# The last head of the first attention stays in SBUF, and the first token block's operands are made inside the attention

## The chip, the cores and the metric

The kernel runs on one core of a Trainium2 chip. The metric is the device time of one execution in microseconds (us). A core has a matrix engine (PE, with its weight loads as PEld), a vector engine (DVE), a scalar engine (ACT), a general engine (POOL), and queues that issue transfers (DMAs) between the chip's large memory (HBM) and the on-chip memory (SBUF); nearly all of this kernel's transfers are issued from SyncE's queue (SP). Matmul results land in PSUM, banks of 128 x 512 float32.

## The reference, cut to what matters

The program is a two-layer encoder over 1024 tokens of width 1024. Layer 0 mixes tokens by multi-head latent attention, layer 1 by differential attention; each mixer and each SwiGLU is followed by a scaled residual and a layer norm. The change lies between the first attention and its output projection:

```python
def block(args):                                # 128 queries at a time, 8 heads
    i, qn_b, qr_b = args
    logits = (jnp.einsum('bqhd,bkhd->bhqk', qn_b, k_nope) + jnp.einsum('bqhd,bkd->bhqk', qr_b, k_rope))
    logits = jnp.where(_chunk_mask(i * Q_BLOCK, s), logits * scale, NEG_BIG)
    p = jax.nn.softmax(logits, axis=-1)
    return jnp.einsum('bhqk,bkhd->bqhd', p, v)
...
o = _from_blocks(o).reshape(b, s, MLA_HEADS * MLA_V)
return o @ w_o
...
h = _layernorm(ALPHA * h + mix, ln_mix_g[i], ln_mix_b[i])
```

## The kernel before, in words

**Numbers.** Every float32 matmul is made of three matmuls of a shorter format: an operand is split into a high part (a cast on ACT) and a low part (a subtraction on DVE or POOL), and the product is high x high + high x low + low x high (`mm3`, lines 143 to 145). So each operand costs a cast and a subtraction before PE can use it.

**The first attention** goes head by head over eight query blocks of 128 tokens. For a block, `softmax_block` makes the scores on PE (s_a, line 216), adds the mask and takes the extreme on DVE (line 219), takes the exponential on ACT (line 222), and POOL multiplies by the reciprocal of the sum (line 1145); all of this lies in a tile `l` of a pool of four buffers. `transpose_block` then transposes the block on PE into PSUM (pt, line 148), and splits it into pth (ACT, line 243) and ptl (DVE, line 244). For two blocks together, `pv_group` multiplies with the values (o_a, line 255; a group g is the pair of blocks 2g and 2g+1), and `mix_a` copies the result out of PSUM (ob, ACT, line 1155) and stores it to HBM (o_dr, line 1156). The last head, head 7, takes its blocks in the order `LAST_ORDER` = 6, 7, 4, 5, 2, 3, 0, 1. A table `fill` names what is done between blocks: projections for the next heads and the like.

**The output projection**, `out_proj`, first loads the eight 128 x 1024 pieces of w_o (r_wo), each split by ACT (line 136) and POOL (line 137). Then, for each token block in `LAST_ORDER`, it fetches all eight heads' outputs of the block from HBM (of, line 299), splits them (ACT line 302, DVE line 303), fetches the block's input rows (zy, line 306), multiplies by w_o (zp_a, 48 matmuls of 128 x 512), adds the residual (line 314), and does the layer norm, whose rows mg and mb POOL's own queue fetches (line 152). Meanwhile the first feed-forward weights (gp) are fetched and split (op_gp, lines 474 and 475).

**What sets the order.** The program is recorded once, and a planner that simulates a time line then fixes one order of instructions for each engine and each DMA queue, so far as the data allow. On the chip each engine works through its list in that order: an instruction that waits holds up those behind it on its engine. A tile's buffer is taken over by the next tile when all readers of the old one are done. In the planned order, the fetch of the first block (block 6) stands on SP behind head 7's store of the group of blocks 6 and 7; the split of block 6's operands stands on ACT ahead of the last pth casts of blocks 0 to 3, and on DVE ahead of their last ptl subtractions; PE's last groups o_a for blocks 2, 3 and 0, 1 need those, and the projection's first matmul stands behind both groups.

Of the kernel before, what the change touches and what calls it, by code (L numbers as in the profile page):

```python
# [9 lines left out]
F32 = mybir.dt.float32  # L10
# [6 lines left out]
P = 128  # L17
# [25 lines left out]
def trunk(  # L43
# [234 lines left out]
    def out_proj(side, w_o, o_dram, x_src, x_dst, lng, lnb, xo):  # L278


        with tc.tile_pool(name="op0", bufs=2, side=side, reuse_waits="tile") as pool:
            g = bcast_row(pool, lng, D, "mg0", "g")
            b = bcast_row(pool, lnb, D, "mb0", "b")
            wo = []
            for h in range(H):
                dst = ()
                if h in (0, 1, 2, 3, 7):
                    t = big_tile(f"wo0_{h}")
                    dst = (t[:, 0], t[:, 1])
                elif h == 6:  # L290
                    t = pool.tile([P, 2, D], F32R, tag=f"wo{h}", name=f"wo0_{h}", bufs=1)
                    dst = (t[:, 0], t[:, 1])
                wo.append(load_w(w_o[h], 1024, f"wo0_{h}", *dst))
            prev = None
            for tb in LAST_ORDER:
                nm = f"a0_{tb}"
                of = pool.tile([P, H, P], F32, tag="of", name=f"of_{nm}", bufs=2)
                src = o_dram[tb // 2][:, :, (tb % 2) * P:(tb % 2) * P + P]
                nc.sync.dma_start(of, src.rearrange("h p q -> p h q"))
                ot = pool.tile([P, 2, D], F32R, tag="oh", name=f"oh_{nm}").rearrange("p a (h q) -> p a h q", h=H)  # L300
                oh, ol = ot[:, 0], ot[:, 1]
                A.copy(oh, of)
                V.tensor_tensor(ol, of, f32(oh), ALU.subtract)
# [757 lines left out]

    with ast as st:
# [88 lines left out]
        def mix_a(h, g):  # L1151
            hc = slice((h % 2) * P, (h % 2) * P + P)
            po = pv_group(pts.pop((h, g)), g, lambda j: tuple(v[:, hc] for v in vt[h // 2, j]), f"a{h}_{g}")
            ob = vp.tile([P, 256], F32, tag="ob", name=f"ob{h}_{g}", bufs=2)
            A.copy(ob, po[:, :256])
            nc.sync.dma_start(o_dr[0][g][h], ob)

# [24 lines left out]
        at(12, constants)  # L1182
        attention(score_a, turn_a, mix_a, fill, 2, (0, 0))
# [13 lines left out]
    def next_x():  # L1197
        pool = xst.enter_context(tc.tile_pool(name="xp0", bufs=1, side="right", reuse_waits="tile"))
        wts["v", 0] = [load_w(w_b_v[0, kh], 1024, f"wbv0_{kh}") for kh in range(2)]
        return new_xT(pool, "f0")  # L1200

    xo, stacks = x_pools("m0", "right")
    pending = out_proj("left", w_o_a, o_dr[0], x, xs_dr[0], ln_mix_g[0], ln_mix_b[0], xo)
# [289 lines left out]
```

## Time and profile before

| | us |
|---|---|
| median of three runs | 2299.32 |
| lowest and highest | 2297.55, 2300.04 |
| the profiled execution | 2302.24 |
| its span, from the first to the last instruction | 2300.2 |
| PE busy | 2253.4 |
| DVE busy | 1551.7 |
| ACT busy | 1017.8 |
| POOL busy | 863.9 |
| first matmul of the output projection, from the span's start | 353.69 |

A profile's row in a timeline gives the start in us, the length in us, the engine, the line of the kernel, the operation, what it writes and reads, shapes and count, and in brackets how long its engine had been idle and who ended that. In a table of stretches each engine has its busy time and, in brackets, the number of its instructions; then come the clock granted to PE (1.00 is full), the DMA engines' busy share, and GB/s. Names are the program's, without buffer numbers: pth_a is the high part of a transposed block of the first attention.

### The profile page before, as it was taken

Reading aid. Unit: us, or ns where it says so; the run is one execution under the profiler, and the core shown is the slowest. Engines: PE = TensorE matmul, PEld = TensorE weight load, DVE = VectorE, ACT = ScalarE, POOL = GpSimd, SP = SyncE. Lnnn points to the kernel's source line nnn. Section 1 sums busy time; section 2 is a strip of 40 time slices with the busy share of each in tenths; the row PEclk is TensorE's granted clock in tenths of the full one; section 3 lists DMA queues with packets and bytes.
Section 4 is the critical chain, followed back from the end, with each engine's and each line's share of the span. In section 5 each row is a group of like instructions: output and inputs, shape, how many; then the busy total and the mean of one; then the engine's idle time right before and its main releaser. Section 6 shows DMA issues by size and latency. Waiting matters only on the chain. (4 is left out here: it accounts for less than half of the span.)

```text
span 2300.2 us, 31168 instructions
## 1 busy us (share of the span) xinstructions
PE 2253.4 (98%) x11410; PEld 1919.6 (83%) x11410; DVE 1551.7 (67%) x2891; ACT 1017.8 (44%) x2096; POOL 863.9 (38%) x688
## 2 busy tenths in 40 slices
PE   8999999999999999999999999999999999999997
PEld 8899997878888887888888898987778888887886
DVE  5667664596666668667476667576586666658777
ACT  4455573342333324445365656555442333324453
POOL 2223241014444445555432424221014444435564
PEclk9999999999999999999999999999999999999999
DMA  5010125434435338544310212053344232337453
GB/s 200 14 36 30 41 72 180 138 128 142 178 133 197 128 111 327 198 171 156 94 54 19 70 38 69 16 214 139 108 160 149 76 120 87 125 127 284 160 205 121
DMA packets 105545, 288.28 MB, mean 125 GB/s; under 512 B 7968, under 2 KB 30112, under 8 KB 94896
## 3 DMA queue, kind: packets, MB, share of 16 engines
q1 hardware_dynamic: 100976, 275.87, 33.5%
q0 software_dynamic: 4416, 10.42, 1.7%
q8 instruction: 90, 1.47, 0.3%
q14 instruction: 63, 0.52, 0.1%
HBM read 205.00 MB, written 77.07 MB: 123 GB/s over the span
## 5 line engine op out<-in xcount | busy, mean ns | idle before, releaser
L474 ACT CAST op_g<-gr 128x512 fp32r<-128x512 f32 x240 | 147.0, 621 | 376.5 <-PE gb L520 188.4
L475 POOL TENSOR_TENSOR op_g<-gr,op_g 128x512 fp32r<-128x512 f32 x104 | 144.0, 1390 | 254.2 <-ACT op_g L474 140.7
L475 DVE TENSOR_TENSOR op_h<-rh,op_h 128x512 fp32r<-128x512 f32 x154 | 157.8, 1055 | 68.2 <-ACT op_h L474 68.2
L520 PE MATMUL ga<-xh_m,op_g 128*128 128x512 f32 x512 | 168.1, 389 | 0.0
L474 ACT CAST op_h<-rh 128x512 fp32r<-128x512 f32 x154 | 92.7, 619 | 147.5 <-PE dx L790 41.1
L790 PE MATMUL dw<-op_w_t,op_h 128*128 128x512 f32 x660 | 151.1, 390 | 0.0
L790 PEld LDWEIGHTS dw<-op_w_t,op_h 128*128 128x128 f32 x660 | 123.6, 188 | 25.6
L222 ACT ACTIVATE l_b<-l_b,mx_b 128x256 f32<-128x256 f32 (+7 forms) x128 | 99.5, 778 | 78.9 <-DVE mx_b L219 77.1
L1297 POOL TENSOR_SCALAR l_b<-l_b,r_b,cst 128x128 f32<-128x128 f32 (+3 forms) x64 | 52.8, 824 | 204.1 <-DVE r_b L224 193.5
L790 PE MATMUL dx<-op_w_b,op_h 128*128 128x512 f32 x528 | 124.4, 397 | 5.0 <-ACT op_w_b L474 3.9
L475 POOL TENSOR_TENSOR op_w_t<-tt,op_w_t 128x512 fp32r<-128x512 f32 x66 | 98.6, 1497 | 80.5 <-ACT op_w_t L474 79.9
L790 PEld LDWEIGHTS dx<-op_w_b,op_h 128*128 128x128 f32 x528 | 101.1, 192 | 28.0 <-ACT op_w_b L474 4.7
L475 DVE TENSOR_TENSOR op_g<-gr,op_g 128x512 fp32r<-128x512 f32 x136 | 111.4, 821 | 17.6 <-ACT op_g L474 17.4
L520 PE MATMUL gc<-b22h_f,op_g 128*128 128x512 f32 x352 | 115.6, 389 | 2.5 <-ACT op_g L474 2.5
L520 PE MATMUL gb<-t3h_f,op_g 128*128 128x512 f32 x352 | 115.6, 390 | 2.2 <-ACT tmp L622 1.6
L520 PE MATMUL gb<-t4h_f,op_g 128*128 128x512 f32 x352 | 115.8, 390 | 1.3 <-DVE tmp L603 1.3
L475 POOL TENSOR_TENSOR op_g<-s,op_g 128x512 fp32r<-128x512 f32 x40 | 54.6, 1365 | 166.0 <-ACT op_g L474 158.0
L520 PE MATMUL gc<-t1h_f,op_g 128*128 128x512 f32 x352 | 115.9, 390 | 0.6 <-ACT op_g L474 0.5
L520 PE MATMUL gb<-t2h_f,op_g 128*128 128x512 f32 x352 | 115.2, 390 | 0.4 <-DVE op_g L475 0.4
L520 PEld LDWEIGHTS ga<-xh_m,op_g 128*128 128x128 f32 x512 | 96.1, 188 | 20.0
L143 PE MATMUL bp<-xT_f,h_wb 128*128 128x512 f32 x256 | 103.7, 405 | 0.0
L145 PE MATMUL bp<-xT_f,l_wb 128*128 128x512 f32 x256 | 102.0, 399 | 0.0
(376 smaller groups left out, 6749.6 us busy)
## 6 DMA issues: line engine op xcount, KB each, us to landing
gr<-in_w_gu SPq DMA_DIRECT2D x44, 1024.0 KB, 6.9
rh<-h_dr SPq DMA_DIRECT2D x28, 1024.0 KB, 5.1
h_dr<-sh SPq DMA_DIRECT2D x22, 1024.0 KB, 5.0
h_dr<-hp SPq DMA_DIRECT2D x22, 768.0 KB, 4.1
tt<-in_w_dn SPq DMA_DIRECT2D x22, 512.0 KB, 7.9
rh<-h_dr SPq DMA_DIRECT2D x14, 768.0 KB, 4.3
wo_dr<-op_pwo SPq DMA_DIRECT2D x16, 512.0 KB, 3.4
z<-xs_dr SPq DMA_DIRECT2D x16, 512.0 KB, 10.1
```

The lines of the kernel that those rows point to most:

```text
L143: T.matmul(ps_out, lh, rh, start=(i == 0), stop=False)
L145: T.matmul(ps_out, ll, rh, start=False, stop=(i == n - 1))
L222: A.activation(l[:, :n], l[:, :n], AF.Exp, bias=mx, scale=-1.0, accum_out=sm)
L474: A.copy(hi, src)
L475: eng.tensor_tensor(lo, src, f32(hi), ALU.subtract)
L520: T.matmul(o, w[:, a, kc], x[b][:, k, :], start=(first and k == 0 and (a, b) == (0, 0)), stop=(k == 3 and a == 1), skip_group_check=True,)
L790: T.matmul(o, h[:, a, c], w[:, b_], start=(first and (a, b_) == (0, 0)), stop=(last and a == 1), skip_group_check=True,)
L1297: G.tensor_scalar(l1[:, :n], l1[:, :n], r1, nlam, ALU.mult, ALU.mult)
```

## The change

Head 7's result is no longer stored to HBM and fetched again: `mix_a` copies it to a tile `o_last` (128 x 1024) that lives until the feed-forward takes its place. The fetch of a token block brings seven heads, and `split_rows` is called twice a block, once for the seven heads and once for head 7's piece of `o_last`. For the first block in `LAST_ORDER`, block 6, the fetch and the split of the seven heads are moved into the attention: `first_rows` is put into the table `fill` at slot 59, after head 7's block 5. Its raw rows take a buffer of the pool of `l`, its operands (ohh, ohl) those of the weight pool `wp`. The first six pieces of w_o are recorded there as well, ahead of that fetch; pieces 6 and 7 stay in `out_proj`.

In the planned order of the changed kernel, the fetch for block 6 stands on SP behind head 6's last store. On ACT, the seven heads' cast for block 6 stands after the first pth cast of block 5 and ahead of its other two and of the cast of w_o's piece 7. POOL splits piece 7 ahead of normalising block 0. Block 7's operands now stand ahead of the last pth cast and ptl subtraction of blocks 0 and 1; PE's order stays nearly as it was.

```diff
@@ -275,32 +275,39 @@
                 fn()
         mix(blocks[-1][0], blocks[-1][1] // 2)
 
-    def out_proj(side, w_o, o_dram, x_src, x_dst, lng, lnb, xo):
+    def split_rows(ot, of, hs):
+        oh, ol = (t[:, hs] for t in ot)
+        A.copy(oh, of)
+        V.tensor_tensor(ol, of, f32(oh), ALU.subtract)
+
+    def load_wo(h, pool=None):
+
+        if h in (4, 5):
+            return load_w(w_o_a[h], 1024, f"wo0_{h}")
+        t = big_tile(f"wo0_{h}") if pool is None else pool.tile([P, 2, D], F32R, tag="wo", name=f"wo0_{h}", bufs=1)
+        return load_w(w_o_a[h], 1024, f"wo0_{h}", t[:, 0], t[:, 1])
+
+    def out_proj(side, wo, o_dram, o_last, first, x_src, x_dst, lng, lnb, xo):
 
 
         with tc.tile_pool(name="op0", bufs=2, side=side, reuse_waits="tile") as pool:
             g = bcast_row(pool, lng, D, "mg0", "g")
             b = bcast_row(pool, lnb, D, "mb0", "b")
-            wo = []
-            for h in range(H):
-                dst = ()
-                if h in (0, 1, 2, 3, 7):
-                    t = big_tile(f"wo0_{h}")
-                    dst = (t[:, 0], t[:, 1])
-                elif h == 6:
-                    t = pool.tile([P, 2, D], F32R, tag=f"wo{h}", name=f"wo0_{h}", bufs=1)
-                    dst = (t[:, 0], t[:, 1])
-                wo.append(load_w(w_o[h], 1024, f"wo0_{h}", *dst))
+            wo = wo + [load_wo(6, pool), load_wo(7)]
             prev = None
             for tb in LAST_ORDER:
                 nm = f"a0_{tb}"
-                of = pool.tile([P, H, P], F32, tag="of", name=f"of_{nm}", bufs=2)
-                src = o_dram[tb // 2][:, :, (tb % 2) * P:(tb % 2) * P + P]
-                nc.sync.dma_start(of, src.rearrange("h p q -> p h q"))
-                ot = pool.tile([P, 2, D], F32R, tag="oh", name=f"oh_{nm}").rearrange("p a (h q) -> p a h q", h=H)
-                oh, ol = ot[:, 0], ot[:, 1]
-                A.copy(oh, of)
-                V.tensor_tensor(ol, of, f32(oh), ALU.subtract)
+                if tb == LAST_ORDER[0]:
+                    ot = first
+                else:
+                    of = pool.tile([P, H, P], F32, tag="of", name=f"of_{nm}", bufs=2)[:, :H - 1]
+                    src = o_dram[tb // 2][:H - 1, :, (tb % 2) * P:(tb % 2) * P + P]
+                    nc.sync.dma_start(of, src.rearrange("h p q -> p h q"))
+                    ot = pool.tile([P, 2, D], F32R, tag="oh", name=f"oh_{nm}").rearrange("p a (h q) -> p a h q", h=H)
+                    ot = ot[:, 0], ot[:, 1]
+                    split_rows(ot, of, slice(0, H - 1))
+                split_rows(ot, o_last[:, tb * P:(tb + 1) * P], H - 1)
+                oh, ol = ot
                 zy = pool.tile([P, 2, D], F32, tag="zy", name=f"zy_{nm}")
                 z, y = zy[:, 0], zy[:, 1]
                 nc.sync.dma_start(z, x_src[tb * P:(tb + 1) * P, :])
@@ -1059,6 +1066,10 @@
         V.tensor_scalar(nlam, nlam, -LAMBDA_INIT, None, ALU.add)
 
 
+    obst = ExitStack()
+    o_last = obst.enter_context(tc.tile_pool(name="obp", bufs=1, side="right")).tile(
+        [P, S], F32, tag="olast", name="o_last")
+    wo0, first = [], []
     with ast as st:
         pool = st.enter_context(tc.tile_pool(name="a1", bufs=2, reuse_waits="tile"))
         vp = st.enter_context(tc.tile_pool(name="a1v", bufs=12, side="right", reuse_waits="tile"))
@@ -1151,9 +1162,26 @@
         def mix_a(h, g):
             hc = slice((h % 2) * P, (h % 2) * P + P)
             po = pv_group(pts.pop((h, g)), g, lambda j: tuple(v[:, hc] for v in vt[h // 2, j]), f"a{h}_{g}")
+            if h == H - 1:
+                A.copy(o_last[:, g * 256:g * 256 + 256], po[:, :256])
+                return
             ob = vp.tile([P, 256], F32, tag="ob", name=f"ob{h}_{g}", bufs=2)
             A.copy(ob, po[:, :256])
             nc.sync.dma_start(o_dr[0][g][h], ob)
+
+        def first_rows():
+
+
+            wo0.extend(load_wo(h) for h in range(6))
+            tb = LAST_ORDER[0]
+            of = lp.tile([P, H, P], F32, tag="l", name="of_a0_first")[:, :H - 1]
+            src = o_dr[0][tb // 2][:H - 1, :, (tb % 2) * P:(tb % 2) * P + P]
+            nc.sync.dma_start(of, src.rearrange("h p q -> p h q"))
+            first.append([
+                wp.tile([P, D], F32R, tag=f"w{p}", name=f"oh{p}_a0_first").rearrange("p (h q) -> p h q", h=H)
+                for p in "hl"
+            ])
+            split_rows(first[0], of, slice(0, H - 1))
 
         fill = {}
 
@@ -1180,6 +1208,7 @@
             at(b + (6 if h < H - 1 else 4), q_nope, h, 1)
             at(b + (7 if h < H - 1 else 5), k_nope, h, 1)
         at(12, constants)
+        at(8 * H - 5, first_rows)
         attention(score_a, turn_a, mix_a, fill, 2, (0, 0))
 
     banks("ps2", PS_BUFS)
@@ -1195,12 +1224,13 @@
     xst, wts = ExitStack(), {}
 
     def next_x():
+        obst.close()
         pool = xst.enter_context(tc.tile_pool(name="xp0", bufs=1, side="right", reuse_waits="tile"))
         wts["v", 0] = [load_w(w_b_v[0, kh], 1024, f"wbv0_{kh}") for kh in range(2)]
         return new_xT(pool, "f0")
 
     xo, stacks = x_pools("m0", "right")
-    pending = out_proj("left", w_o_a, o_dr[0], x, xs_dr[0], ln_mix_g[0], ln_mix_b[0], xo)
+    pending = out_proj("left", wo0, o_dr[0], o_last, first[0], x, xs_dr[0], ln_mix_g[0], ln_mix_b[0], xo)
 
     def split_wo(h, c):
 
```

## The prediction

> **What bounds the kernel now.** I read the page's busy table, then PE's clock and busy time stretch by stretch around the place of the change, then PE's waits there, then the timeline of each engine. The page:
>
> ```profile
> span 2300.2 us, 31168 instructions
> ...
> PE 2253.4 (98%) x11410; PEld 1919.6 (83%) x11410; DVE 1551.7 (67%) x2891; ACT 1017.8 (44%) x2096; POOL 863.9 (38%) x688
> ```
>
> TensorE is busy 98% of the span, so only what makes PE wait, or run at a lower clock, costs time. The hand-over from the first attention to its output projection (first projection matmul at 353.69 us) is such a place. The stretches (columns: length; busy PE, PEld, DVE, ACT, POOL; granted clock; DMA share; GB/s):
>
> ```profile
> 347.00:351.00 4.00, 1.50 (x9) 0.85 (x7) 2.78 (x2) 2.13 (x5) 2.83 (x3) 0.91 0.95 333
> 351.00:354.00 3.00, 2.50 (x11) 2.50 (x12) 0.78 (x3) 0.37 (x1) 0.00 (x0) 0.50 1.06 349
> 354.00:357.00 3.00, 3.00 (x8) 2.32 (x8) 1.22 (x1) 1.45 (x3) 0.00 (x0) 0.50 1.03 406
> ...
> 365.00:445.00 80.00, 80.00 (x379) 66.79 (x378) 43.11 (x79) 26.05 (x52) 3.87 (x7) 1.00 0.33 112
> ```
>
> Between 347 and 354 PE is idle 3 us, and its clock is halved until about 357 (a mean of 0.91 from 347 to 351 puts the drop near 350.3). From 365 to 445 it never pauses: nothing that the change does to later token blocks can show unless it makes PE wait. PE's waits between 340 and 360, and its rows there (start, length, work, [idle before, and who ended it]):
>
> ```profile
> PE o_a L255 <- ACT pth_a L243: 1.9, 2, 1.5
> PE o_a L255 <- DVE ptl_a L244: 1.1, 1, 1.1
> ```
> ```profile
> 339.21 0.27 PE L148 MATMUL pt_a<-ident,l_a 128*128 128x128 f32 x1
> ...
> 343.33 0.28 PE L255 MATMUL o_a<-pth_a,vl 128*128 128x256 f32 x1
> ...
> 344.20 0.38 PE L255 MATMUL o_a<-pth_a,vh 128*128 128x256 f32 x1
> ...
> 348.95 0.39 PE L255 MATMUL o_a<-pth_a,vh 128*128 128x256 f32 x1 [1.45 <-ACT pth_a L243]
> ...
> 351.50 0.58 PE L255 MATMUL o_a<-ptl_a,vh 128*128 128x256 f32 x1 [1.09 <-DVE ptl_a L244]
> ...
> 352.63 0.52 PE L255 MATMUL o_a<-ptl_a,vh 128*128 128x256 f32 x1
> ...
> 353.69 0.73 PE L143 MATMUL zp_a<-wo,oh_a 128*128 128x512 f32 x1
> ...
> 357.16 0.40 PE L145 MATMUL zp_a<-wo,oh_a 128*128 128x512 f32 x1
> 357.40 0.39 PE L143 MATMUL zp_a<-wo,oh_a 128*128 128x512 f32 x1
> ```
>
> Who made PE wait stands in the rows of ACT, DVE, POOL and the DMA queue:
>
> ```profile
> 341.10 0.37 ACT L1155 COPY ob<-o_a 128x256 f32<-128x256 f32 x1 [0.59 <-PE o_a L255]
> 341.56 0.37 ACT L243 CAST pth_a<-pt_a 128x256 fp32r<-128x256 f32 x1
> 342.18 0.40 ACT L222 ACTIVATE l_a<-l_a,mx_a 128x128 f32<-128x128 f32 x1 [0.25 <-DVE mx_a L219]
> ...
> 342.58 0.35 ACT L243 CAST pth_a<-pt_a 128x256 fp32r<-128x256 f32 x1
> 342.83 1.05 ACT L136 CAST wo<-r_wo 128x1024 fp32r<-128x1024 f32 x1
> 343.78 0.65 ACT L243 CAST pth_a<-pt_a 128x256 fp32r<-128x256 f32 x2
> 344.30 0.53 ACT L222 ACTIVATE l_a<-l_a,mx_a 128x256 f32<-128x256 f32 x1
> ...
> 344.81 1.05 ACT L136 CAST wo<-r_wo 128x1024 fp32r<-128x1024 f32 x1
> ...
> 347.14 1.05 ACT L302 CAST oh_a<-of_a 128x1024 fp32r<-128x1024 f32 x1 [0.85 <-DMA of_a<-o_dr]
> ...
> 348.36 0.54 ACT L243 CAST pth_a<-pt_a 128x128 fp32r<-128x128 f32 x2
> ```
> ```profile
> 348.22 2.69 DVE L303 TENSOR_TENSOR oh_a<-of_a,oh_a 128x1024 fp32r<-128x1024 f32 x1 [1.44 <-ACT oh_a L302]
> 350.84 0.94 DVE L244 TENSOR_TENSOR ptl_a<-pt_a,pth_a 128x128 fp32r<-128x128 f32 x3
> 355.20 1.22 DVE L303 TENSOR_TENSOR oh_a<-of_a,oh_a 128x1024 fp32r<-128x1024 f32 x1 [3.42 <-ACT oh_a L302]
> ```
> ```profile
> 343.03 0.38 POOL L1145 TENSOR_SCALAR l_a<-l_a,r_a 128x128 f32<-128x128 f32 x1 [1.62 <-PE pt_a L148]
> 343.53 0.59 POOL L152 DMA_DIRECT2D mg<-in_ln_mix_g  x1
> ...
> 344.68 2.39 POOL L137 TENSOR_TENSOR wo<-r_wo,wo 128x1024 fp32r<-128x1024 f32 x1
> 347.04 0.47 POOL L1145 TENSOR_SCALAR l_a<-l_a,r_a 128x256 f32<-128x256 f32 x1
> 347.49 2.34 POOL L137 TENSOR_TENSOR wo<-r_wo,wo 128x1024 fp32r<-128x1024 f32 x1
> ```
> ```profile
> 341.49 0.33 SPq L1156 DMA_DIRECT2D o_dr<-ob  x1
> 343.24 0.38 SPq L299 DMA_DIRECT2D of_a<-o_dr  x1
> ```
>
> ACT's cast of the first block's rows (347.14) waits for their fetch, which waits for head 7's store (341.49). Behind that cast stand the pth casts that PE needs. DVE's subtraction takes 2.69 us, where the same one later takes 1.22, and the ptl rows that PE needs stand behind it.
>
> **The change part by part.** The planner's order, engine by engine, is the same up to this hand-over, and after it but for the split casts.
>
> *Removed.* Four stores of head 7 (SP). Nothing on PE waits for them once the fetches no longer do: 0.
>
> *Fetch of the first block, seven heads.* It now waits for head 6's store, long landed, and for its buffer: that of block 4's scores, free after the transpose at 339.21 (end 339.48). So it issues at 339.5, against 343.24. Issue to landing of all sixteen such fetches in the two layers:
>
> ```profile
> DMA to landing us min/median/max: 3.4/4.4/20.0
> ```
>
> The 343.24 fetch of eight heads took 3.9 to its cast; nothing large is in flight ahead of the new one, so I take 3.8: it lands at 343.3 (bounds 342.9 to 343.9).
>
> *ACT: the wait moves forward.* The new cast stands ahead of three things that PE's next group needs: pth for block 5 (two casts) and wo 7's cast. ACT copies head 7 at 341.1, casts its piece, casts pth (as at 341.56), and then has to wait from about 341.9 to 343.3. The cast of 896 columns steps 0.84 (0.95, from 342.83 to 343.78, times 7/8), the next pth 0.25 (342.58 to 342.83), wo 7 0.95; the pth that PE takes at 344.20 is then cast at 345.35 and done at 345.7. PE idles from 343.6 to 345.75: 1.55 us later than before.
>
> *What it wins.* The exponentials and weight cast keep their lengths (0.40, 0.51, 0.95); with the pair of pth casts and block 7's last-head piece (0.17) between, the last pth of block 3 is done at 349.1 (348.9 before), but now DVE has no long subtraction ahead: its ptl is ready at 349.55 against about 351.5. From ptl to the end of that group (o_a for blocks 2 and 3) are five steps, 1.13 at half clock (351.50 to 352.63): it ends at 350.2 at full clock; at half, the 17 matmuls ahead (0.22 each from 346.6, with the transposes) last until 350.3 and it ends at 351.5. Before it ended near 352.6.
>
> *What the tail gives back.* Before, the last group's pth and ptl were made ahead of block 7's operands. Now ACT has, between the end of the group before and the last pth, the copy to the kept tile (step 0.26), the 896 cast for block 7 (0.84), a 128 cast (0.17) and then pth (0.27): 1.5 us. DVE has block 7's subtraction (1.22 x 7/8 = 1.07), a 128 one (0.29) and ptl (0.29). At full clock the cast is done at 351.4, but POOL holds its split of wo 6 until 352.35, and in the 2.69 row DVE stood until POOL's split had ended (349.83) and then took 1.1. POOL's order is wo 7 from 345.5 (2.39), block 0's scores (0.38), two DMA issues (1.15, from 343.53 to 344.68), block 1's scores (0.47), wo 6 (2.34). I charge that wait: the subtraction ends at 353.4, ptl at 354.0. At half clock: cast 352.7, ptl 354.3. From ptl to the first projection matmul was 1.06 (352.63 to 353.69): 355.1 to 355.4, against 353.69. I take +1.5.
>
> *Clock.* The eight steps from 353.69 to 357.16 took 3.47; at 0.24 (357.16 to 357.40) they are 1.92: 1.55 lost. PE had worked steadily for 5.5 us (351.50 to 357) when the clock came back. Steady work now starts at 354.0, so it comes back at 359.5; 4.3 us of projection at half speed lose 2.15: +0.6. The bounds are no loss at all (-1.55) and a recovery as long as the whole slow stretch of before, 6.7 us (350.3 to 357): +1.2.
>
> [...]
>
> *Queues and buffers.* Block 0's scores wait for block 5's transposes in place of block 4's, for their buffer, and for POOL's wo 7: normalised at 348.3, ahead of the last pth of block 3: 0. SP issues the next fetches and the input rows earlier, behind the first fetch. The casts of the first feed-forward weights now wait until block 6's matmuls free their buffer, and take the place that block 4's cast had:
>
> ```profile
> 366.45 1.06 ACT L302 CAST oh_a<-of_a 128x1024 fp32r<-128x1024 f32 x1 [8.34 <-PE zp_a L145]
> ```
> ```profile
> 372.08 0.32 SPq L184 DMA_DIRECT2D xs_dr<-zy_a  x1
> ```
>
> The weight fetch that waits for them on SP stands ahead of this store of block 6's result, which comes later anyway: 0.
>
> *Split casts for the other blocks.* Seven times one ACT and one DVE instruction more (0.27 and 0.29), under the 80 us in which PE never pauses; ACT has 54 us free there, DVE 37: 0. Were that cover gone, 3.9.
>
> **Sum.** +1.5 + 0.6 = +2 us on an execution of 2302.24 (span 2300.2 and 2.0 around it), which is 0.13% over the median 2299.32; by that median, 2301.3. Low end: the fetch lands before ACT gets there (-1.4) and the clock is never halved under the projection: 1.5 - 1.4 - 1.55 = -1.5. High end: landing at 343.9 (+0.6) and the long recovery: 1.5 + 0.6 + 1.2 = +3.3.
>
> **Rivals.** *Slower: a small subtraction caught behind POOL.* Block 7's last-head subtraction now stands ahead of the ptl that PE needs, due at 348.8; POOL takes wo 6 at 350.0. If ACT falls 1.2 us behind POOL there, DVE is held as in the 2.69 row, until 352.35; ptl comes at 353.1 instead of 349.55, and +3.5 joins the +2: 2304.8. The margin speaks against it; that ACT hangs on a DMA, and that its order is woven with four engines', speaks for it. [...]
>
> *Slower: the fetch late.* Each us after 343.3 costs one; from 345.9 on it passes 0.2%. The fetch of 343.24 and its 3.9 us speak against it, the 20.0 for it: some 2305.
>
> *Faster: the stall simply goes.* The 3.0 us of idling and the clock's loss (1.55, and half of the 2.2 from 351.50 to 353.69) vanish: -5.6, 2293.7. For it: the fetch and the 2.69 subtraction do leave the place. Against it: block 7's casts take the same place, and they stand ahead of the last pth and ptl in the planner's order.
>
> *It does nothing:* the end of the group stays at 353.7 by chance: 2299.3, within my range.
>
> **How the numbers follow.** Forecast +2 (with the no-effect case) 0.63, caught subtraction or late fetch 0.27, stall gone 0.10. Run medians scatter by about 1 us around this, so the range is 2296.5 to 2306.0; the likeliest case alone has 2297.5 to 2303.7. About 0.2% (4.6 us) is what a measurement of this kernel can tell from no change: faster 0.10, same 0.63, slower 0.27.
>
> **What would show it.** Right: the fetch issues near 339.5; an ACT wait of over 1 us for it; a PE wait of about 2 us near 343.6; another on the last pth and ptl near 351 to 354; the first projection matmul near 355.2; the clock back near 360; no PE wait from there to 445. Wrong: the projection starting before 352, or after 358; or a wait anywhere beyond the hand-over.

## The result, and the profile after

The changed kernel takes 2302.79 us in the median of 11 runs (2300.46 to 2307.23), the kernel before, run beside it, 2297.99 us (2296.42 to 2302.13). The ratio is 1.0023, with a 95% interval of 1.0015 to 1.0030: some 5 us slower, just past the 0.2% that I had called measurable. I had forecast +2 us. The profiled execution took 2302.16 us with a span of 2300.2, by chance the span of the profiled execution of before, which was a high one of its kernel (2302.24 against the median of 2297.99); so the two traces are compared at the hand-over and not by their ends.

The page of the changed kernel, PE's waits between 340 and 362, and three of the stretches (columns as before):

```profile
PE 2250.8 (98%) x11410; PEld 1917.4 (83%) x11410; DVE 1559.0 (68%) x2899; ACT 1018.8 (44%) x2104; POOL 867.1 (38%) x688
```
```profile
PE o_a L255 <- ACT pth_a L243: 3.9, 3, 2.2
PE o_a L255 <- DVE ptl_a L244: 3.8, 2, 3.2
```
```profile
351.00:354.00 3.00, 1.25 (x6) 1.25 (x7) 1.90 (x3) 0.00 (x0) 1.21 (x1) 0.50 0.89 363
354.00:357.00 3.00, 1.11 (x4) 0.42 (x3) 1.64 (x4) 2.52 (x5) 0.00 (x0) 0.50 0.02 10
...
365.00:445.00 80.00, 80.00 (x379) 66.75 (x378) 41.82 (x83) 26.63 (x58) 7.37 (x9) 1.00 0.30 103
```

The operand waits of PE at the hand-over grew from 3.0 us (1.9 and 1.1) to 7.7. Between 351 and 357, PE now works 2.4 us of 6, where it worked 5.5. From 365 to 445 it still never pauses. So the whole effect lies here, at the hand-over and in the projection's first matmuls. The rows, of the queue, ACT, PE, DVE and POOL:

```profile
339.59 0.39 SPq L1179 DMA_DIRECT2D of_a_first<-o_dr  x1
```
```profile
343.31 0.94 ACT L280 CAST ohh_a_first<-of_a_first 128x896 fp32r<-128x896 f32 x1 [1.21 <-DMA of_a_first<-o_dr]
...
347.59 1.05 ACT L136 CAST wo<-r_wo 128x1024 fp32r<-128x1024 f32 x1
...
354.12 0.37 ACT L1166 COPY o_last<-o_a 128x256 f32<-128x256 f32 x1 [4.57 <-PE o_a L255]
```
```profile
345.80 0.39 PE L255 MATMUL o_a<-pth_a,vh 128*128 128x256 f32 x1 [2.16 <-ACT pth_a L243]
...
349.16 0.39 PE L255 MATMUL o_a<-pth_a,vh 128*128 128x256 f32 x1 [0.42 <-ACT pth_a L243]
...
352.75 0.58 PE L255 MATMUL o_a<-ptl_a,vh 128*128 128x256 f32 x1 [3.21 <-DVE ptl_a L244]
...
357.05 0.58 PE L255 MATMUL o_a<-ptl_a,vh 128*128 128x256 f32 x1 [0.61 <-DVE ptl_a L244]
...
358.18 0.73 PE L143 MATMUL zp_a<-wo,ohh_a_first 128*128 128x512 f32 x1
...
361.18 0.40 PE L144 MATMUL zp_a<-wo,ohh_a_first 128*128 128x512 f32 x1
```
```profile
348.87 3.50 DVE L281 TENSOR_TENSOR oh_a<-o_last,oh_a 128x128 fp32r<-128x128 f32 x1 [0.97 <-ACT oh_a L280]
352.29 0.61 DVE L244 TENSOR_TENSOR ptl_a<-pt_a,pth_a 128x256 fp32r<-128x256 f32 x2
355.36 1.09 DVE L281 TENSOR_TENSOR oh_a<-of_a,oh_a 128x896 fp32r<-128x896 f32 x1 [2.46 <-ACT oh_a L280]
356.37 0.28 DVE L281 TENSOR_TENSOR oh_a<-o_last,oh_a 128x128 fp32r<-128x128 f32 x1
```
```profile
348.84 0.55 POOL L152 DMA_DIRECT2D mb<-in_ln_mix_b  x1
349.42 0.49 POOL L1156 TENSOR_SCALAR l_a<-l_a,r_a 128x256 f32<-128x256 f32 x1
349.87 2.34 POOL L137 TENSOR_TENSOR wo<-r_wo,wo 128x1024 fp32r<-128x1024 f32 x1
```

Read it from the DVE rows. The subtraction of block 7's last head is 128 x 128; at 356.37 the same form takes 0.28 us, at 348.87 it takes 3.50 and ends 0.16 after POOL's split of wo 6 (349.87 + 2.34 = 352.21). Below, a DVE instruction that is held like this until a split of POOL has ended is called caught. The ptl of block 3 stands behind it, PE waits 3.21 us for that ptl, ACT waits 4.57 for PE's group before it goes on to block 7's cast, and so the projection starts at 358.18 in place of 353.69. This is the rival "a small subtraction caught behind POOL", which I had priced at 2304.8, 5.5 us over the kernel before.

Against the trace of before, an execution as a whole is shifted by up to 1 us before it comes to this place. The experiments are therefore measured from a mark, block 5's exponential on ACT, ahead of all work on the engines that the edits move (in e5, e8 and e10 the first fetches are issued before it), to the first projection matmul and to the second residual addition of block 6, which ends the part that the edits touch. For before and after the mark and the end are these rows:

```profile
335.89 0.94 ACT L222 ACTIVATE l_a<-l_a,mx_a 128x768 f32<-128x768 f32 x1
...
366.45 0.69 DVE L314 SCALAR_TENSOR_TENSOR zy_a<-zy_a,zp_a 128x512 f32<-128x512 f32 x1 [4.74 <-PE zp_a L145]
```
```profile
335.92 0.94 ACT L222 ACTIVATE l_a<-l_a,mx_a 128x768 f32<-128x768 f32 x1
...
370.71 0.69 DVE L321 SCALAR_TENSOR_TENSOR zy_a<-zy_a,zp_a 128x512 f32<-128x512 f32 x1 [4.74 <-PE zp_a L145]
```

| kernel | mark to projection, us | against before | mark to residual, against before | ratio of times to the kernel before, run beside it, 95% interval |
|---|---|---|---|---|
| before | 17.80 | | (30.56) | |
| changed | 22.26 | +4.46 | +4.23 | 1.0023 (1.0015 to 1.0030) |
| e1_small_behind | 18.92 | +1.12 | +1.05 | 1.0006 (0.9996 to 1.0016) |
| e2_block7_behind | 16.80 | -1.00 | -2.58 | 0.9988 (0.9979 to 0.9997) |
| e3_wo6_late | 18.68 | +0.88 | -0.70 | 1.0003 (0.9994 to 1.0012) |
| e4_first_behind | 20.50 | +2.70 | +2.47 | 1.0006 (0.9997 to 1.0014) |
| e5_kept_only | 19.21 | +1.41 | +0.36 | 1.0010 (1.0001 to 1.0020) |
| e6_both | 18.10 | +0.30 | -0.27 | 0.9998 (0.9989 to 1.0007) |
| e7_wo67_late | 16.22 | -1.58 | -2.16 | 0.9987 (0.9978 to 0.9996) |
| e8_fetch_early | 14.73 | -3.07 | -4.64 | 0.9985 (0.9976 to 0.9993) |
| e10_fetch_early_a4 | 14.22 | -3.58 | -5.17 | 0.9977 (0.9968 to 0.9986) |
| e12_wo6_ready_later | 18.49 | +0.69 | -0.90 | 1.0007 (0.9998 to 1.0016) |

0.0010 is 2.3 us, about the half width of an interval; within 2.5 us the time follows the distance to the residual in every row, and rows that lie closer together than that are told apart by their distances alone. e11_more_issues ran once, for its trace, and has no ratio. Where the two columns of distance differ, it is the halved clock (0.50 from 354 to 357 in the kernel before and the changed one): whether the projection's first matmuls still run under it. The first of them takes 0.73 or 0.74 us in the kernel before, the changed one, e1, e4, e5, e6 and e7, and 0.44 or 0.45 us in e2, e3, e8, e10 and e12, whose second column lies 1.6 us lower than their first.

### The profile page after: what moved, and what is told of

It is laid out like the page before. It is cut to its first block, busy times and chain, and to the rows that moved or that the text cites. A ratio compares the mean times of both kernels' runs of the same rounds, so it can differ in the third digit from the quotient of the medians.

```text
span 2300.2 us, 31162 instructions
## 1 busy us (share of the span) xinstructions
PE 2250.8 (98%) x11410; PEld 1917.4 (83%) x11410; DVE 1559.0 (68%) x2899; ACT 1018.8 (44%) x2104; POOL 867.1 (38%) x688
## 5 line engine op out<-in xcount | busy, mean ns | idle before, releaser
L482 DVE TENSOR_TENSOR op_h<-rh,op_h 128x512 fp32r<-128x512 f32 x154 | 162.5, 1086 | 64.0 <-ACT op_h L481 64.0
```

Source lines behind the costliest of these rows:

```text
L482: eng.tensor_tensor(lo, src, f32(hi), ALU.subtract)
```

## The experiments

Theory 1: the small subtraction, held by POOL, made the loss, and DVE held by POOL bounds this hand-over altogether. Theory 2, the rival: the wait for the early fetch (2.16 us of PE) and the order of the tail made it. In the edits, `behind(i, j)` sets instruction i behind j in the planned order without a wait of its own; `marks[b]` holds the pth and ptl instructions of block b. The edits shift the line numbers: 243 and 244 become 245 and 246, 255 becomes 258, 280 and 281 become 283 and 284 (two more in e11).

### The small subtraction moved, or POOL's split moved

e1_small_behind puts the one small piece of block 7 behind block 3's pth and ptl:

```diff
-    def split_rows(ot, of, hs):
+    def split_rows(ot, of, hs, after=None):
...
+        if after is not None:
+            for mh, ml in marks[after]:
+                behind(i.ins, mh)
+                behind(j.ins, ml)
...
-                split_rows(ot, o_last[:, tb * P:(tb + 1) * P], H - 1)
+                split_rows(ot, o_last[:, tb * P:(tb + 1) * P], H - 1, "a7_3" if tb == LAST_ORDER[1] else None)
```

e2_block7_behind puts all pieces of blocks 7 and 4 behind those of block 1:

```diff
-                    split_rows(ot, of, slice(0, H - 1))
-                split_rows(ot, o_last[:, tb * P:(tb + 1) * P], H - 1)
+                    split_rows(ot, of, slice(0, H - 1), "a7_1" if tb in LAST_ORDER[1:3] else None)
+                split_rows(ot, o_last[:, tb * P:(tb + 1) * P], H - 1, "a7_1" if tb in LAST_ORDER[1:3] else None)
```

e3_wo6_late leaves ACT, DVE and PE as they are and makes POOL's split of wo 6 wait for block 1's last ptl:

```diff
-            wo = wo + [load_wo(6, pool), load_wo(7)]
+            w6 = pool.tile([P, 2, D], F32R, tag="wo", name="wo0_6", bufs=1)
+            split6 = load_w(w_o_a[6], 1024, "wo0_6", w6[:, 0], w6[:, 1], ins=True)[1]
+            tc.add_manual_dep(
+                split6, marks["a7_1"][-1][1].name,
+                mybir.DependencyInfo(mybir.DependencyClass.Sync, mybir.DependencyReason.DATA), reason="behind the last ptl")
+            wo = wo + [(w6[:, 0], w6[:, 1]), load_wo(7)]
```

> Edit: block 7's last-head piece (one cast, one subtraction of 128x128) is put behind block 3's last pth and ptl; nothing else moves. Theory 1 (the small subtraction of 3.50 us at 348.87, held by POOL, made the loss): block 3's ptl is done by about 349.7, and the group o_a of blocks 2 and 3 ends near 351; the tail of the prediction stays (block 7's long subtraction waits for POOL's split of wo 6, which ends at 352.2), so the first projection matmul starts at 354.6 to 355.4 instead of 358.18, about 3 us earlier, and the time is 0 to 3 us over the kernel before. Theory 2 (the wait of ACT for the early fetch and the order of the tail made it): the small subtraction only changes places, the projection starts at 357 or later and the time stays 4 us or more over the kernel before.

> Edit: all splits of blocks 7 and 4 are put behind the last pth and ptl of blocks 0 and 1. Theory 1 and the tail term together: no subtraction from SBUF stands ahead of a ptl between 347 and 353; block 3's ptl is done by 349.7, that of blocks 0 and 1 by about 352.2, and the projection starts at 351.7 to 353.0: 5 to 6 us earlier than in the changed kernel, 1 to 2 earlier than in the kernel before, and the time is 3 us below to 1 us over the kernel before. Theory 2 with the fetch as the main cost: PE still waits 2.16 us at 343.6 and the projection starts no earlier than 354.5, since what comes late there stays late.

> Edit: POOL's split of wo 6 waits for the last ptl of blocks 0 and 1; the order on ACT, DVE and PE is that of the changed kernel. Theory 1: the small subtraction still starts near 348.9 and is not held to 352.4. If a DMA issue on POOL does not hold DVE it takes 0.3 us; if it does, it ends near 349.4 (end of the issue) or 349.9 (end of block 1's scores, the next instruction). Block 3's ptl is then done at 349.5 to 350.5, block 7's long subtraction is not held either, and the projection starts at 353.8 to 355.0, 3 to 4 us earlier than in the changed kernel; the time is 0 to 2 us over the kernel before. Theory 2: the projection starts at 357 or later, since fetch and tail are as they were; and if POOL's split is needed early, PE waits for wo 6 in the projection.

DVE and POOL in e1, DVE in e3, and PE in e2:

```profile
348.30 0.42 DVE L246 TENSOR_TENSOR ptl_a<-pt_a,pth_a 128x256 fp32r<-128x256 f32 x1 [1.04 <-ACT pth_a L245]
348.64 3.08 DVE L284 TENSOR_TENSOR oh_a<-o_last,oh_a 128x128 fp32r<-128x128 f32 x1
```
```profile
349.21 2.35 POOL L137 TENSOR_TENSOR wo<-r_wo,wo 128x1024 fp32r<-128x1024 f32 x1
```
```profile
348.77 0.29 DVE L284 TENSOR_TENSOR oh_a<-o_last,oh_a 128x128 fp32r<-128x128 f32 x1 [0.97 <-ACT oh_a L283]
```
```profile
344.93 0.48 PE L258 MATMUL o_a<-pth_a,vh 128*128 128x256 f32 x1 [2.11 <-ACT pth_a L245]
...
351.90 0.44 PE L143 MATMUL zp_a<-wo,ohh_a_first 128*128 128x512 f32 x1
```

All three came out as theory 1 said, in time and, to 0.4 us (e1 starts that much earlier than its range), in the start of the projection (354.20, 351.90, 353.99); in none of them was the early fetch touched. In e1 the subtraction is caught again (3.08 us, to 0.16 behind POOL's 351.56), but now behind block 3's ptl: the place of one small piece is worth 3.3 us at the projection. In e3 all orders on ACT, DVE and PE are the changed kernel's and only POOL's split is away: 0.29 us in place of 3.50, 3.6 us at the projection. With no subtraction of blocks 7 and 4 ahead of a ptl (e2), PE still waits 2.11 us for the fetch, and yet the kernel beats the one before. So the wait for the fetch is not the loss; what it costs on its own shows where it is taken away, in e8 and e10 below.

### Part 1 alone

```diff
-        at(8 * H - 5, first_rows)
...
-            wo = wo + [load_wo(6, pool), load_wo(7)]
+            wo = [load_wo(h, pool if h == 6 else None) for h in range(H)]
...
-                if tb == LAST_ORDER[0]:
-                    ot = first
-                else:
+                if True:
```

> Edit: part 1 of the change alone: head 7 is kept in o_last and every fetch brings seven heads, but the first block is fetched and split in the output projection as in the kernel before. In the planned order its fetch waits for head 6's last store only, so ACT should not wait for it at all, and the cast stands behind wo 6's cast. On DVE the last-head subtraction of block 6 now stands ahead of two ptl, just when POOL starts on its splits of wo 7 and wo 6 (344.7 to 349.8 in the kernel before, with one normalisation between). Theory 1 (DVE held by POOL is what bounds this hand-over, in the kernel before too): that small subtraction takes 3 us or more, block 6's long subtraction comes behind POOL's last split again, and the projection starts at 353.2 to 355.2, so no gain: 1 us below to 2 us over the kernel before. Theory 2 (the fetch bounds it): without the wait for the fetch the projection starts at 352 or earlier, and the time is 2 us or more below the kernel before.

The queue, ACT, DVE and POOL:

```profile
334.67 0.38 SPq L303 DMA_DIRECT2D of_a<-o_dr  x1
```
```profile
346.52 0.96 ACT L280 CAST oh_a<-of_a 128x896 fp32r<-128x896 f32 x1
```
```profile
346.24 3.90 DVE L281 TENSOR_TENSOR oh_a<-o_last,oh_a 128x128 fp32r<-128x128 f32 x1 [0.97 <-ACT oh_a L280]
350.07 0.61 DVE L244 TENSOR_TENSOR ptl_a<-pt_a,pth_a 128x256 fp32r<-128x256 f32 x2
```
```profile
344.84 2.40 POOL L137 TENSOR_TENSOR wo<-r_wo,wo 128x1024 fp32r<-128x1024 f32 x1
347.19 0.49 POOL L1154 TENSOR_SCALAR l_a<-l_a,r_a 128x256 f32<-128x256 f32 x1
347.64 2.35 POOL L137 TENSOR_TENSOR wo<-r_wo,wo 128x1024 fp32r<-128x1024 f32 x1
```

Keeping head 7 does take the fetch off the path: it is issued at 334.67 instead of 343.24 and ACT waits for nothing at its cast. The gain is nil: by the rows, the new 128 x 128 subtraction is held for 3.90 us, from the midst of one split of POOL to the end of the next, and PE then waits 3.6 us for the ptl behind it. No run moved that subtraction alone in this kernel. The projection starts at 355.26 and the time is 2.3 us over the kernel before, both just past the upper end of what theory 1 gave; theory 2 had wanted 352 and 2 below.

### The first block's operands moved, and what met them

e4_first_behind puts the seven-head split of block 6 behind block 5's pth and ptl. e6_both is that and e2_block7_behind. e7_wo67_late is e6_both, with the wait of e3_wo6_late on both of POOL's last splits:

```diff
-            split_rows(first[0], of, slice(0, H - 1))
+            split_rows(first[0], of, slice(0, H - 1), "a7_5")
```
```diff
+            for h in (6, 7):
...
+                tc.add_manual_dep(
+                    split, marks["a7_1"][-1][1].name,
```

> Edit: the first block's seven-head cast and subtraction are put behind block 5's last pth and ptl, so that ACT has work while the fetch is under way; the early fetch stays. Both theories: PE's wait of 2.16 us near 343.6 goes, and ACT and POOL run 1 to 2 us earlier from there. Theory 1: that alone wins little, since the small subtraction still stands ahead of block 3's ptl and now starts near 347.8, in the midst of POOL's two DMA issues and ahead of its split of wo 6 (now about 349.0 to 351.4): if it is held to that end, block 3's ptl comes at 351.7 and the projection starts at 353.5 to 355; if a DMA issue does not hold it, at 350.5 to 351.5. Theory 2: the wait for the fetch was the loss, so the whole hand-over moves 2.2 us or more forward, with the 3.50 us subtraction no longer on the path; projection at 351 or earlier, time 3 us or more below the kernel before.

> Edit: blocks 7 and 4 behind the last ptl (as in e2_block7_behind) and the first block's operands behind block 5's (as in e4_first_behind). Theory 1, by the rows of those two: the first block's long subtraction is caught behind POOL's split of wo 7 again (2.28 us there), block 0's normalisation and the transposes behind it wait for it near 347, and that gives back what the fetch's wait gave; no subtraction stands ahead of the last ptl, so the projection starts at 351.0 to 352.3, as with blocks 7 and 4 behind alone (351.90): 2 to 4 us below the kernel before, no further than that kernel. If instead the edits add up, it starts below 350.5 and the time is 5 us or more below.

> Edit: as e6_both, and POOL's splits of wo 6 and wo 7 wait for the last ptl of blocks 0 and 1, so that no subtraction of DVE before the projection meets a split of POOL. Theory 1: every subtraction of DVE from 342 to the last ptl keeps its usual length (1.09 for 896 columns, 0.3 for 128), block 0 is normalised 1.3 us earlier than with the first block behind alone (346.91), and the projection starts at 349.3 to 350.8, without slow matmuls ahead; wo 6 is needed 4.2 us after the start (18 matmuls of 0.23), wo 7 at 5.6, and POOL takes 2.4 each, up to 3.2 beside DVE: a wait of PE in the projection of up to 1.5 us. The time is 3 to 6 us below the kernel before. If DVE held by POOL were not what bounds this place, the start would be as in e6_both and the waits for wo 6 and wo 7 a loss on top.

DVE, POOL, ACT and PE in e4:

```profile
344.12 2.28 DVE L284 TENSOR_TENSOR ohl_a_first<-of_a_first,ohh_a_first 128x896 fp32r<-128x896 f32 x1 [0.41 <-ACT ohh_a_first L283]
...
348.94 2.54 DVE L284 TENSOR_TENSOR oh_a<-o_last,oh_a 128x128 fp32r<-128x128 f32 x1 [0.97 <-ACT oh_a L283]
```
```profile
343.06 2.39 POOL L137 TENSOR_TENSOR wo<-r_wo,wo 128x1024 fp32r<-128x1024 f32 x1 [2.35 <-ACT wo L136]
...
348.99 2.34 POOL L137 TENSOR_TENSOR wo<-r_wo,wo 128x1024 fp32r<-128x1024 f32 x1
```
```profile
347.68 1.03 ACT L136 CAST wo<-r_wo 128x1024 fp32r<-128x1024 f32 x1
```
```profile
347.34 0.33 PE L148 MATMUL pt_a<-ident,l_a 128*128 128x128 f32 x1 [1.88 <-POOL l_a L1163]
```

The 2.16 us wait for the fetch is gone in e4, and a wait of 1.88 takes its place. The subtraction of 896 columns now comes 1.06 us after POOL took wo 7; it is held to that split's end (345.45), takes 2.28, block 0's reciprocal stands behind it, POOL's normalisation behind that, and PE's transposes last. The last-head subtraction is caught as well (2.54 us). So little is won, as theory 1 had it (1.4 us over the kernel before, where theory 2 had 3 or more below), but the projection starts at 355.70, 0.7 past its range, since I had foreseen the catch of the small subtraction and not that of the long one.

I sized e6 and e7 too early, by 1 to 2 us. e6 was to start as e2 does, between 15.9 and 17.2 after the mark (351.0 to 352.3, e2's 351.90 being 16.80); it starts at 18.10, and its time is that of the kernel before, where 2 to 4 us below were expected. The catch of 2.27 us at DVE came as expected; not reckoned with was PE's clock, halved in its last groups (0.58 us for an o_a matmul that takes 0.38 in e2). In e7 every subtraction ahead of the last ptl has its usual length (1.09 us for 896 columns, 0.29 for 128) and block 0 is normalised 1.1 us earlier than in e4 (10.59 after the mark against 11.71), and PE never waits for wo 6 or wo 7; but the projection starts 16.22 after the mark, not 14.2 to 15.7, at half clock again (its first matmul takes 0.73 us, in e2 0.44), and the time is 3.0 us below the kernel before, the least of what theory 1 gave.

### The early fetch made early in earnest

e8_fetch_early is e2_block7_behind with the first of these edits, e10_fetch_early_a4 has both:

```diff
-            of = lp.tile([P, H, P], F32, tag="l", name="of_a0_first")[:, :H - 1]
+            of = f32(pool.tile([P, S], F32R, tag="kn0", name="of_a0_first")).rearrange("p (h q) -> p h q", h=H)[:, :H - 1]
...
-            split_rows(first[0], of, slice(0, H - 1))
+            split_rows(first[0], of, slice(0, H - 1), "a7_4")
```

> Edit: as e2_block7_behind, and the first block's rows land in the buffer of head 6's keys, free long before, in place of that of block 4's scores. The fetch then waits only for head 6's last store; with part 1 alone it was issued at 334.67, so it lands near 338.5. The planner puts the cast on ACT ahead of block 2's exponential (337.7 in the changed kernel), so ACT may wait up to 1 us for the landing there. If the fetch still cost its 2.1 us of PE's wait near 343 in e2_block7_behind, that wait goes and the projection starts 1 to 2 us earlier after block 3's exponential than there (13.15 us after it): 11 to 12.3, and the time is 3.5 to 6 us below the kernel before. If that wait was only shifted to 337.5 or to the last transposes, the start stays at 12.5 to 13.5 and the time at 2 to 4 below.

> Edit: as e8_fetch_early, with the first block's seven-head cast and subtraction put behind block 4's last pth and ptl (340.3 to 341.1 in the changed kernel), so that nothing waits for the landing at 338.5 and POOL has no split under way (its split of wo 7 starts at 343 or later). Theory 1: the subtraction of 896 columns takes 1.09 us, PE has no wait of over 1 us between 340 and 350, and the projection starts 10.5 to 12 us after block 3's exponential (14.15 before, 18.61 in the changed kernel): 4 to 6 us below the kernel before. If the subtraction is caught all the same, or another wait takes the place of the fetch's, 12.5 or later, as in e2_block7_behind.

The queue, ACT, DVE and PE in e10:

```profile
334.04 0.38 SPq L1186 DMA_DIRECT2D of_a_first<-o_dr  x1
```
```profile
339.86 0.94 ACT L283 CAST ohh_a_first<-of_a_first 128x896 fp32r<-128x896 f32 x1
```
```profile
340.83 1.09 DVE L284 TENSOR_TENSOR ohl_a_first<-of_a_first,ohh_a_first 128x896 fp32r<-128x896 f32 x1 [0.55 <-ACT ohh_a_first L283]
```
```profile
349.57 0.44 PE L143 MATMUL zp_a<-wo,ohh_a_first 128*128 128x512 f32 x1
```

The buffer of block 4's scores had held the fetch back until 339.59. In the buffer of head 6's keys it is issued 1.3 us ahead of the mark instead of 3.7 behind it, nothing waits for its landing, its subtraction meets no split, and PE's longest operand wait is 0.5 us. The projection starts 10.58 us after block 3's exponential (338.99 in this execution), within the 10.5 to 12 expected. e10 has the lowest time here: 0.9977 of the kernel before (0.9968 to 0.9986), 5 us faster than it and, by the two ratios, some 10 faster than the changed kernel; its interval overlaps that of e8. In e8 the planner's own place for the cast, ahead of block 2's exponential, made ACT wait 0.82 us for the landing. With the cast itself ahead of it too, block 3's exponential came 5.15 us after the mark instead of 3.64, so the projection's distance from there (9.58, where 11 to 12.3 was expected) says too little, and the table's mark is the one to read: by it e8 starts 2.07 us earlier than e2, where 1 to 2 was expected. Its time, 3.4 us below, is at the edge of the gain expected. e8's edit differs from e2's in the fetch's buffer alone (the planner then moved the cast), so the late fetch cost e2 about 2 us.

The loss of the changed kernel is thus theory 1's. Its claim that DVE held by POOL bounds this place altogether does not hold: in e7 no DVE instruction is held ahead of the last ptl, and yet its projection starts 2.0 us later after the mark than that of e10, where the fetch is early as well.

### What holds the subtraction: the issue, the split, or the split to come

In the changed kernel the subtraction started 1.0 us before the split that it was held by, within a DMA issue of POOL.

e11_more_issues is e3_wo6_late with the layer norm's two rows fetched in halves, which makes four issues out of two:

```diff
-        nc.gpsimd.dma_start(t, src.partition_broadcast(P))
+        for c in range(2 if name in ("mg0", "mb0") else 1):
+            cs = slice(c * n // 2, (c + 1) * n // 2) if name in ("mg0", "mb0") else slice(0, n)
+            nc.gpsimd.dma_start(t[:, cs], src[cs].partition_broadcast(P))
```

e12_wo6_ready_later is the changed kernel with e3's wait aimed at an earlier instruction, ACT's last pth of block 3:

```diff
-                split6, marks["a7_1"][-1][1].name,
+                split6, marks["a7_3"][-1][0].name,
```

> Edit: as e3_wo6_late (no split of POOL in reach), and the two rows of the layer norm are fetched in halves, so that POOL issues four DMAs of about 0.55 us each, from about 347.7 to 349.9, and DVE's last-head subtraction for block 7 starts in their midst (348.8 in that kernel, 0.04 us ahead of the end of the second issue). If an issue of POOL alone holds the subtraction, it takes 0.6 us or more, up to 1.2 to the end of the issues; if an issue does not, and only the split does, 0.3 us. The time itself tells nothing here.

> Edit: the changed kernel, with one wait more: POOL's split of wo 6 also waits for ACT's last pth of block 3, the cast right behind the one that releases the caught subtraction (done at 349.1 in the changed kernel, where the split starts at 349.87 and its operands were ready at 348.6). Orders are unchanged, and POOL should not be late by it. In the changed kernel the subtraction started at 348.87, 1.0 us ahead of that split, and was held all the same; with the split far off (e3_wo6_late, e11_more_issues) it took 0.29 within POOL's DMA issues. If a split that is only ready, behind the issues and block 1's normalisation, already holds DVE, the subtraction now takes 0.3 us, since the split is not ready when it starts; the split starts as before, block 7's long subtraction meets it or just misses it, and the projection starts 15 to 16 us after block 3's exponential, 0 to 2 us over the kernel before. If what counts is only that a split follows closely on POOL, the subtraction is held to the split's end again (2.5 us or more) and the start is at 18 or later, 4 us or more over the kernel before.

DVE and POOL in e11; then DVE, ACT and POOL in e12:

```profile
348.38 0.29 DVE L286 TENSOR_TENSOR oh_a<-o_last,oh_a 128x128 fp32r<-128x128 f32 x1 [0.97 <-ACT oh_a L285]
```
```profile
347.54 1.13 POOL L154 DMA_DIRECT2D mg<-in_ln_mix_g  x2
```
```profile
348.21 0.29 DVE L284 TENSOR_TENSOR oh_a<-o_last,oh_a 128x128 fp32r<-128x128 f32 x1 [0.97 <-ACT oh_a L283]
```
```profile
348.08 0.38 ACT L245 CAST pth_a<-pt_a 128x256 fp32r<-128x256 f32 x1
```
```profile
347.82 0.54 POOL L152 DMA_DIRECT2D mb<-in_ln_mix_b  x1
348.40 0.49 POOL L1168 TENSOR_SCALAR l_a<-l_a,r_a 128x256 f32<-128x256 f32 x1
348.85 2.37 POOL L137 TENSOR_TENSOR wo<-r_wo,wo 128x1024 fp32r<-128x1024 f32 x1
```

In e11 the subtraction lies within POOL's issues (348.38 to 348.67, in 347.54 to 348.67) and takes its 0.29: an issue alone does not hold it. e12 is the changed kernel with one more wait on POOL, which delays POOL by nothing: its split follows the normalisation at once, 0.64 us after the subtraction's start, closer than in the changed kernel. And the subtraction takes 0.29 in place of 3.50; the projection starts 14.84 us after block 3's exponential (338.70), 0.2 earlier than expected of that case, and the time is 1.6 us over the kernel before. What differs is that the split could start, as far as the work that it waits for goes, before the subtraction started in the changed kernel (348.64, the end of ACT's cast at 347.59), and in e12 0.25 us after (348.46, the end of ACT's pth). So what held DVE there is a split that could start and only stood behind POOL's own issues and normalisation.

The catches of e1 and e4 bear this out. Here are ACT's cast of wo 6 and POOL's second issue in e1:

```profile
346.95 1.05 ACT L136 CAST wo<-r_wo 128x1024 fp32r<-128x1024 f32 x1
```
```profile
348.19 0.54 POOL L152 DMA_DIRECT2D mb<-in_ln_mix_b  x1
```

e1's subtraction (348.64) lies almost as e12's does: it begins 0.09 us ahead of the end of that issue (0.15 in e12) and 0.57 us ahead of the split (0.64 in e12). But there the split was ready at 348.00, and the subtraction took 3.08 us. In e4 the small subtraction begins at 348.94, 0.05 us ahead of a split that was ready at 348.71, and takes 2.54.

## Why the prediction was right and wrong

The time fell inside the range (2296.5 to 2306.0), but the likeliest case was not what happened. The projection started at 358.18, and "after 358" was one of my own signs of being wrong. That 2302.79 lies even within the bounds of the likeliest case alone (2297.5 to 2303.7) is luck: the kernel before, run beside it, took 2297.99 and not the 2299.32 that I added to, so +5 us landed where +3.5 would have. Those bounds also do not follow from the sum: -1.5 and +3.3 on 2299.32 are 2297.8 and 2302.6, or 2296.8 and 2303.6 with the 1 us of scatter. Step by step:

- *The fetch* issued at 339.59 (forecast 339.5) and was there at 343.31 (343.3). *ACT* waited for it (1.21 us, forecast 1.4), and *PE* began the next group at 345.80 after 2.16 us (345.75, "1.55 us later than before"). These sizes hold to 0.2 us.
- *"Its ptl is ready at 349.55"* is the step that failed. PE had block 3's pth at 349.16, as forecast, but the ptl came at 352.75, since the small subtraction ahead of it was held. I had seen the rival and set its condition too narrowly: "if ACT falls 1.2 us behind POOL", because POOL takes wo 6 at 350.0 and the subtraction is due at 348.8. Both times were right (349.87, 348.87). The margin of 1.0 us was still there, and did not help: by e12 a split that is ready can hold DVE before its row begins (3.50 us with the split of the changed kernel, ready 0.23 us ahead of the subtraction's start, and 0.29 with that of e12, ready 0.25 us behind it). The rival's price, +3.5 on top of the rest, is the 3.3 that e1 gives back and the 3.6 that e3 does.
- *The tail, +1.5*: without the catch (e1) the projection starts 1.12 us later than before. Right in kind, 0.4 too large.
- *The clock, +0.6* was wrong in sign: seven slow steps from 358.18 to 361.18 lose 1.4 us (3.0 less 7 of 0.23), against 1.55 before. Full clock was back 4.1 us after PE's last wait (357.05), not 5.5. How much is lost is not fixed by the work: e3 and e11 reach the projection within 0.4 us of each other (353.99, 354.34), e3 at full clock (its first matmul takes 0.44 us) and e11 at half (0.73), and e11 then needs 2.3 us more to the residual. That the clock comes back after 5.5 us of steady work was my estimate from the one stretch of before; what sets the moment no run here shows.
- *Queues, buffers and split casts at 0*: no wait of PE appears from 365 to 445. Right.
- *The rival "the stall simply goes"* needed two things gone: block 7's operands ahead of the last ptl, which I had named against it, and the wait for the fetch, which stood in the sum. e10 takes both away, its projection runs at full clock from the start (a matmul every 0.23 us from 349.85 to 361.90, where the changed kernel has one every 0.43 us from 358.71), and the time falls by 5.3 us by its ratio; I had priced this case at -5.6.

What the sum would have been with the terms as measured: +1.1 for the tail, 3.3 for the catch (both from e1), -0.2 for the clock, 4.2 together; the distance to the residual grew by 4.23 and the time by 3.4 to 6.9.

## What to carry to other kernels

Where a two-input subtraction from SBUF stands on DVE ahead of what PE waits for, look on POOL not only for a split that is running then but for the next one too, if its operands are already there: a margin in start times was none here (1.0 us in the changed kernel, whose subtraction then took 3.50). In this kernel it paid to put such a piece behind the operands that PE waits for, or to give POOL's split one wait more, and a piece of 128 columns cost as much as a long one when it was caught (3.50 us, against 2.69 for the 1024 columns of before). The early fetch was early only with a landing buffer that was free early: the choice of the buffer moved its issue by 5 us, from 3.7 behind the mark to 1.3 ahead of it.

## What the runs showed of the hardware

Every subtraction from SBUF that started at this hand-over while a single split of POOL ran was held until that split had ended: in e4 the one of 896 columns starts at 344.12 and ends at 346.40, 0.95 us after the split's end (345.45); unheld it takes 1.09. Which of the two is held does not go by the rows' starts alone. In the changed kernel DVE's row begins 1.0 us ahead of the split's and loses: it ends 0.16 us after the split (352.37 against 352.21). In e5 DVE's row begins at 346.24 and waits through the end of one split, a normalisation of 0.49 us, and a whole second split, whose operands had been ready since 346.01.

An issue of POOL's DMAs did not hold the subtraction, nor the subtraction the issue: in e11 it takes 0.29 us (348.38 to 348.67) within a pair of issues that takes 1.13 us, where the pair behind it takes 1.06 and POOL's two issues in e10 0.59 and 0.54.

Not held in the same place was a subtraction with one input from PSUM: in e1 the ptl of 348.30, 0.30 us after the split was ready, takes 0.42 us and ends as the caught one begins.

When a split that is only ready holds a subtraction stays open. The account above does not settle the case of splits that stand back to back. In e7 the subtraction of 896 columns got in between two of them (it started at 351.88, 0.32 us after the first, and took 3.00 us; the pair took 5.58 us, where two alone take 4.7). In the kernel before, an addition on DVE with two inputs (822.98, 1.46 us) got in between a running instruction of POOL (822.59 to 823.89) and the next, a split whose cast had ended at 822.40; and a subtraction that started at 1001.92 did not get in between the four splits that ran from 1000.70 to 1005.74: it took 4.39 us, the two behind it 0.68 each.
